# A scheduled two-layer hybrid block: triangular-solve inputs through DRAM, a fused key norm, and a last projection that closes row tile 0 first

## The chip, the cores and the metric

The kernel runs on one NeuronCore of one Trainium2 chip. The metric is device time in microseconds (us) of one execution, as the median of three runs. One further execution was profiled; every row below comes from that one.

## The reference, cut to what matters

Two layers work on 256 latent tokens (stream 1) and, in layer 0 only for the output, 256 context tokens (stream 0); the width is 2048 and everything is float32.

```python
h = rms_norm(x, pre_norm) * (1 + scale) + shift          # adaLN from c
p = split_columns(h @ w_in)                              # one input projection
att = gqa_block_attention(q, keys, vals) * silu(g)       # 8 heads, 8 rows of 128
S = S*w - (S@kk)(kk*a)^T + v k^T ; o = S@r               # RWKV-7 scan, both directions
kk = heads(k * k_k); kk = kk / max(|kk|, 1e-12)
y = concat([att, rwkv, pool]) @ w_out                    # one output projection
x = x + gate * rms_norm(y, post_norm)
```

The scan is computed in chunks of 64 tokens: within a chunk the recurrence becomes a triangular system whose 32x32 diagonal blocks are inverted by elimination.

## The kernel before, in words

The program is written by a scheduler in Python. About twenty workers (generators: `scan`, `front`, `back`, `elim`, `fin`, `att`, `mix`, `main`, `w_split`, `post`, loads ...) yield instructions. `Scheduler.run` keeps a planned clock for each engine, takes the instruction that can start first by that clock (with a priority by worker), and issues it. The order that comes out is fixed: on the chip each engine runs its own list in order and waits at semaphores. All DMAs are issued by SyncE (SP), so SP's list is one queue too.

What the planner believes of a DMA stands in `Engine.call` and `run`: its size is counted in bytes, it holds SP for 60 ns, moves 350 bytes per ns through one pipe, and lands 2900 ns after that (`DMA_LATENCY`); the next engine sees it 130 ns later.

```python
self.free_at["D"] = s + 60
st = max(self.dma_free, s + 60)
self.dma_free = st + op.dur / 350.0
end = self.dma_free + DMA_LATENCY
```

TensorE (PE) carries the projections. Every weight tile `wf` is split into a rounded high part by ScalarE (ACT) and a low part by VectorE (DVE), both in tiles of class `sp`, and each product is made of three matmuls into PSUM (`acc`). `main_in` and `main_out` make these; they have the lowest priority and fill what the other workers leave of PE. Buffers are slots of pools; `CLASSES` gives the most tiles of a class and `PHASES` how many are kept for it at each stage of the run.

Around that runs the RWKV work in 16 units (2 layers x 4 channel groups x 2 streams). `front` makes decays and keys, `back` makes the chunk matrices on PE (`pr<-rf`), masks them on DVE into `UB` (`rb<-pr,c`) and `W`, and copies the diagonal 32x32 blocks with ACT into `N0` (8 copies, `tp<-rb`). `elim` turns `N0` into the layout of the elimination with two DVE transposes into the one tile `DT` (`dt<-tp`), runs 31 steps of a product and an addition (`tp<-dt,tp` and `tp<-tp`), and transposes the result into `T1` and `T2`. `fin` copies those back (`rb<-tp` on ACT) and multiplies them (`pr<-tp,rb` and `pr<-tp` on PE), and `scan` runs the chunks.

The last output projection is `main_out(1, 1, 0)` and `main_out(1, 1, 1)`: 16 k-tiles for columns 0 to 1023 and both row tiles of 128 tokens, then the same for columns 1024 to 2047. `post_work(1, 1)` takes each finished PSUM tile (times the gate on DVE, squares on ACT), and after all eight of them sums the squares, makes the inverse root for both row tiles (12 small DVE steps), then does eight `SCALAR_TENSOR_TENSOR` with the residual and eight stores.

Of the kernel before, what the change touches and what calls it, by code (L numbers as in the profile page):

```python
# [15 lines left out]
ALU = mybir.AluOpType  # L16
# [85 lines left out]
def layout(a):  # L102
# [22 lines left out]
CLASSES = {  # L125
# [15 lines left out]
}  # L141
# [29 lines left out]
def STEPS():  # L171
    into = [[("in", l, g) for g in range(len(GROUPS(l)))] for l in range(DEPTH)]
    out = [("out", 0, 0, 0), ("out", 0, 0, 1), ("out", 0, 1, 0)]
    return into[0] + out + into[1][:EARLY] + [("out", 0, 1, 1)] + into[1][EARLY:] + [("out", 1, 1, 0), ("out", 1, 1, 1)]

# [31 lines left out]
BACK = 60.0  # L207
HELD = 121.75
HOLD = {None: 1000.0, "ada": 3000.0}
# [418 lines left out]
class Hybrid:  # L628
    def __init__(self, ctx, tc, a, log=None):
        self.ctx, self.tc, self.nc, self.a = ctx, tc, tc.nc, a  # L630
        nc = self.nc
        self.V, self.S, self.G = Engine("V", nc.vector), Engine("S", nc.scalar), Engine("G", nc.gpsimd)
        self.T, self.D = Engine("T", nc.tensor), Engine("D", nc.sync)
        pool = lambda n, **kw: ctx.enter_context(tc.tile_pool(name=n, bufs=1, **kw))
        sb, ps = pool("sb"), pool("ps", space=PSUM)
        fixed = sum(n * TILES[t] for t, n in COUNT.items() if t != "p")
        slots = (SB_BYTES - CONST_BYTES - fixed) // TILES["b"]
        tiles = {t: (ps if t == "p" else sb, COUNT.get(t, slots), size) for t, size in TILES.items()}
        self.cp = pool("const")
# [8 lines left out]
        self.ygd = [dram("ygd%d" % l, [4, 128, 512]) for l in range(DEPTH)]  # L648
        self.sch = Scheduler(tiles, CLASSES, log)
        self.sch.set_phase(PHASES["start"])  # L650
        self.flags = set()
        self.now = "start"
        self.count = {}
# [6 lines left out]
    def phase(self, name, after=None):  # L660
        def go():
            if after in (None, self.now):
                self.now = name
                self.sch.set_phase(PHASES[name])
        self.sch.defer(go)

# [167 lines left out]
    def w_loads(self):  # L834
        yield self.until("loaded")
        for kind, l, *at in STEPS()[1:]:
            if kind == "in":
                for q in range(4):
                    for _, _, cb, _, bs in GROUPS(l)[at[0]]:
                        yield from self.w_tile(l, cb, bs, q)  # L840
            else:
                for k in KMIX:
# [275 lines left out]
    def main_work(self):  # L1118
        left = {s: sum(s in STREAMS[m] for g in GROUPS(1) for *_, m, _ in g) for s in range(2)}
        for kind, l, *at in STEPS():  # L1120
            if kind == "in":
                yield from self.main_in(l, at[0], left)
            else:
                yield from self.main_out(l, *at)
# [59 lines left out]
    def main_out(self, l, s, nh):  # L1184
# [19 lines left out]
        if nh == 1:  # L1204
            self.free(*self.mx[l, s][0].values(), *self.mx[l, s][1].values())

    def emit(self, l, kind, i, ps, mode):
# [83 lines left out]
    def fin_work(self):  # L1291
        yield self.until("consts")
        for _ in range(DEPTH * 8):
            yield Until(lambda: len(self.zq) > 0)
            yield from self.fin(*self.zq.pop(0))

    def front(self, l, g, s, up):
# [14 lines left out]

        kr = yield Alloc("tp", (128, 256))
        yield V.tensor_scalar(out=kr, in0=k, scalar1=self.vec(l, "rw_k_k", g), scalar2=None, op0=ALU.mult)
        sq = yield Alloc("tp", (128, 256))
        yield S.activation(out=sq, in_=kr, func=AF.Square)
# [3 lines left out]
        yield V.tensor_tensor(out=kk, in0=kr, in1=psb[:, 0:256], op=ALU.mult)  # L1320
        self.free(kr, psb)

# [90 lines left out]
    def back(self, l, g, s, need, RS, W, BK, PC, bv):  # L1413
# [13 lines left out]
        for d in range(2):  # L1427
# [9 lines left out]
            for p in range(2):  # L1437
# [5 lines left out]
                self.free(psA[p])  # L1443
        N0 = yield Alloc("tp", (128, 2, 4, 32))
        for q in range(4):
            b = q % 2
            for d in range(2):
                yield S.copy(out=N0[Q[q], d], in_=UB[d][Q[q], :, 0, 32 * b:32 * b + 32])
        for d in range(2):
# [4 lines left out]
            self.free(psW)  # L1454
        self.push(self.bq, (N0, (l, g, s, need, RS, W, UB, BK, PC, bv)))

    def elim(self, N0, unit):
        V = self.V
        DT = yield Alloc("dt", (128, 2, 32, 32))
        for d in range(2):  # L1460
            src = N0[:, d].rearrange("p c t -> p t c").unsqueeze(2).to_broadcast([128, 32, 8, 4])
            dst = DT[:, 0].rearrange("p a b -> p b a") if d == 0 else DT[:, 1]
            yield V.transpose(out=dst, in_=src)
        self.free(N0)
# [3 lines left out]
        yield V.tensor_copy(out=ZZ, in_=z0)  # L1468
        for t in range(31, 0, -1):
            m0 = t // 8  # L1470
            M = 4 - m0
            tm = TM[:, 0:2 * t * M].rearrange("p (d a m) -> p d a m", d=2, a=t)
            yield V.tensor_tensor(out=tm, in0=DT[:, :, 0:t, t:t + 1].to_broadcast([128, 2, t, M]),
                                  in1=ZZ[:, :, t:t + 1, m0:4].to_broadcast([128, 2, t, M]), op=ALU.mult)
            yield V.tensor_tensor(out=ZZ[:, :, 0:t, m0:4], in0=ZZ[:, :, 0:t, m0:4], in1=tm, op=ALU.add)
        self.free(DT, TM)
# [9 lines left out]
    def fin(self, T1, T2, l, g, s, need, RS, W, UB, W2, PC, bv):  # L1486
        V, S, G, T = self.V, self.S, self.G, self.T
        for q in range(4):
            b = q % 2
            yield S.copy(out=UB[0][Q[q], :, 0, 32 * b:32 * b + 32], in_=T1[Q[q], 0].rearrange("p c u -> p u c"))  # L1490
            yield S.copy(out=UB[1][Q[q], :, 0, 32 * b:32 * b + 32], in_=T2[Q[q], 1])
        psY = yield Alloc("pr", (128, 512))
        for u in range(4):
            for p in range(2):
                q0, q1 = Q[2 * p], Q[2 * p + 1]
                o = slice(32 * u, 32 * u + 32)
                yield T.matmul(out=psY[q1, o], lhsT=UB[0][q0, u, 0, 32:64], rhs=T2[q0, 0, u, :], start=True, stop=True)
                yield T.matmul(out=psY[q0, o], lhsT=UB[1][q1, u, 0, 0:32], rhs=T1[q1, 1, :, u], start=True, stop=True)
        YS = yield Alloc("tp", (128, 4, 32))
# [3 lines left out]
        for u in range(4):  # L1503
            for p in range(2):
                q0, q1 = Q[2 * p], Q[2 * p + 1]
                o = slice(32 * u, 32 * u + 32)
                yield T.matmul(out=psZ[q0, o], lhsT=YS[q1, u, :], rhs=T1[q1, 0, :, u], start=True, stop=True)
                yield T.matmul(out=psZ[q1, o], lhsT=YS[q0, u, :], rhs=T2[q0, 1, u, :], start=True, stop=True)
        psz3 = psZ[:, 0:128].rearrange("p (u t) -> p u t", u=4)
# [3 lines left out]
        self.free(psZ, YS, T1, T2)  # L1513
        self.push(self.pq, (l, g, s, need, RS, W, UB, W2, PC, bv))

    def scan_work(self):
        yield self.until("consts")
        state = {}
        for _ in range(DEPTH * 8):
# [3 lines left out]
            if u[0:3] == (0, 3, 1):  # L1523
                self.phase("rested", "first")

    def scan(self, Sc, l, g, s, need, RS, W, UB, W2, PC, bv):
# [150 lines left out]
    def att_work(self, first):  # L1677
        yield self.until("consts")
        for l in range(first, DEPTH):
            while self.count.get(("att", l), 0) < 8:  # L1680
# [10 lines left out]
                if self.count["qdone", l, i // 4] == 4:  # L1691
                    self.free(*self.kf[l, i // 4], *self.vf[l, i // 4])

    def gate_work(self):
# [193 lines left out]
    def run(self):  # L1888
# [24 lines left out]
        sch.add("mix", PRIO["mix"], self.mix_work())  # L1913
        for l in range(DEPTH):
            for s in PASSES(l):
                sch.add("post%d%d" % (l, s), PRIO["post"], self.post_work(l, s), 16)
        sch.add("load", PRIO["load"], self.loads())
# [25 lines left out]
```

## Time and profile before

| what | value |
|---|---|
| median of 3 runs | 1725.89 us (1724.2 to 1728.25) |
| the profiled execution | 1729.24 us, of which the span from the first to the last instruction is 1727.4 us |
| PE, DVE, ACT busy | 1657.9, 1348.7, 929.0 us |
| granted TensorE clock | 0.987 of full speed |
| DMA | 349.77 MB, 61.4% of 16 engines' span on SP's queue |

PE is busy in 96% of the span. Of the rest, 18.5 us lie at the start, before the first weights land, and some 13 us at the end, after the last matmul.

### The profile page before, as it was taken

Reading aid. Unit: us, or ns where it says so; the run is one execution under the profiler, and the core shown is the slowest. Engines: PE = TensorE matmul, PEld = TensorE weight load, DVE = VectorE, ACT = ScalarE, POOL = GpSimd, SP = SyncE. Lnnn points to the kernel's source line nnn. Section 1 sums busy time; section 2 is a strip of 40 time slices with the busy share of each in tenths; the row PEclk is TensorE's granted clock in tenths of the full one; section 3 lists DMA queues with packets and bytes.
Section 4 is the critical chain, followed back from the end, with each engine's and each line's share of the span. In section 5 each row is a group of like instructions: output and inputs, shape, how many; then the busy total and the mean of one; then the engine's idle time right before and its main releaser. Section 6 shows DMA issues by size and latency. Waiting matters only on the chain.

```text
span 1727.4 us, 38237 instructions
## 1 busy us (share of the span) xinstructions
PE 1657.9 (96%) x13658; PEld 1336.4 (77%) x13658; DVE 1348.7 (78%) x4250; ACT 929.0 (54%) x2279; POOL 9.3 (1%) x77
## 2 busy tenths in 40 slices
PE   4899999999999999999999999989999999999997
PEld 3677676776777777777777889789999988998885
DVE  4335889898898898854557685899999999999663
ACT  5333454544555555534346574666546757766461
POOL 0000000000000000000000000000000000000000
PEclk9999999999999999999999999999999999999998
DMA  9993763567566655568579964574523554564762
GB/s 330 374 364 104 248 198 102 178 205 230 162 190 184 218 186 182 178 205 297 193 238 361 331 214 156 160 259 142 160 87 125 167 152 150 178 186 151 259 199 98
DMA packets 217822, 349.77 MB, mean 202 GB/s; under 512 B 22880, under 2 KB 61856, under 8 KB 217632
## 3 DMA queue, kind: packets, MB, share of 16 engines
q1 hardware_dynamic: 217632, 347.34, 61.4%
q8 instruction: 107, 1.75, 0.4%
q14 instruction: 83, 0.68, 0.1%
HBM read 316.41 MB, written 30.83 MB: 201 GB/s over the span
## 4 chain that ended last, share of the span: by engine, by line
PE 76%; DVE 10%; DMA 9%; ACT 2%; issue 2%; SPq 1%; DVEq 0%; ACTq 0%
PE acc L588 54%; PE pr L588 6%; PE att L588 6%; PE scan L588 5%; PE ada L588 4%; DVE tp L588 3%; DMA wa<-in_ada_w_dram 2%; DVE sp L588 2%; DMA w<-in_ada_w_dram 2%; DMA wf<-in_w_in_dram 2%; DVE rf L588 1%; DMA pw<-in_w_in_dram 1%; DVE dt L588 1%; PE st L588 1%; SPq L588 1%
## 5 line engine op out<-in xcount | busy, mean ns | idle before, releaser
L588 PE MATMUL acc<-h,sp 128*128 128x256 f32 (+1 forms) x5088 | 971.2, 339 | 11.4 <-DVE h L588 4.3
L588 PEld LDWEIGHTS acc<-h,sp 128*128 128x128 f32 x5088 | 759.1, 189 | 124.9 <-issue 11.6
L588 DVE TENSOR_TENSOR sp<-wf,sp 128x512 fp32r<-128x512 f32 (+1 forms) x568 | 359.4, 661 | 38.0 <-ACT sp L588 31.9
L588 ACT CAST sp<-wf 128x512 fp32r<-128x512 f32 (+1 forms) x624 | 351.3, 604 | 21.5 <-PE acc L588 5.7
L588 PE MATMUL acc<-sp,h 128*128 128x512 f32 x1152 | 278.4, 398 | 0.1
L588 PEld LDWEIGHTS acc<-sp,h 128*128 128x128 f32 x1152 | 215.0, 189 | 50.1 <-DVE sp L588 1.0
L588 DVE TENSOR_TENSOR tp<-tp 128x60 f32<-128x60 f32 (+21 forms) x552 | 134.4, 246 | 7.1 <-ACT tp L588 0.3
L588 DVE TENSOR_TENSOR tp<-dt,tp 128x48 f32<-128x48 f32 (+23 forms) x496 | 111.0, 224 | 6.3
L588 PEld LDWEIGHTS scan<-rf 128*64 128x64 f32 x1344 | 57.2, 138 | 34.6 <-issue 9.5
L588 PE MATMUL scan<-rf 128*64 128x64 f32 x1344 | 78.0, 233 | 1.7 <-DVE rf L588 1.0
L588 PE MATMUL ada<-wa,cs 128*2 128x256 f32 x1024 | 71.9, 378 | 2.5 <-DMA wa<-in_ada_w_dram 2.2
L588 ACT CAST pw<-pw 128x512 fp32r<-128x512 f32 x56 | 34.8, 622 | 65.4 <-DMA pw<-in_w_in_dram 59.8
L588 DVE TENSOR_TENSOR rf<-tp 64x256 f32<-64x256 f32 x176 | 69.2, 419 | 0.2
L588 DVE STREAM_TRANSPOSE dt<-tp 128x1024 f32<-128x1024 f32 x32 | 65.8, 2075 | 0.1
L588 DVE TENSOR_TENSOR pw<-pw 128x512 f32<-128x512 f32 x56 | 38.4, 686 | 34.5 <-ACT pw L588 34.2
L588 ACT ACTIVATE aq<-att,q 128x512 f32<-128x512 f32 (+1 forms) x48 | 34.0, 708 | 57.0 <-DVE q L588 40.7
L588 DVE COPY adasb<-ada 2x128 f32<-2x128 f32 (+1 forms) x32 | 11.4, 357 | 66.0 <-ACT adasb L588 63.9
L588 DVE SCALAR_TENSOR_TENSOR q<-q 128x4 f32<-128x4 f32 (+3 forms) x378 | 56.9, 155 | 3.7
L588 PE MATMUL ada<-w,cs 128*2 128x128 f32 x1024 | 37.5, 295 | 21.2 <-DMA w<-in_ada_w_dram 20.2
L588 ACT COPY rf<-scan 64x128 f32<-64x128 f32 x128 | 33.3, 260 | 44.1 <-PE scan L588 40.6
L588 ACT COPY adasb<-ada 2x128 f32<-2x128 f32 (+1 forms) x32 | 9.9, 309 | 87.2 <-PE ada L588 83.7
L588 ACT COPY sm<-scan 128x128 f32<-128x128 f32 x64 | 17.1, 267 | 69.6 <-PE scan L588 69.1
(153 smaller groups left out, 1936.6 us busy)
## 6 DMA issues: line engine op xcount, KB each, us to landing
wf<-in_w_in_dram SPq DMA_DIRECT2D x384, 256.0 KB, 3.6
wa<-in_ada_w_dram SPq DMA_DIRECT2D x256, 256.0 KB, 4.6
wf<-in_w_out_dram SPq DMA_DIRECT2D x192, 256.0 KB, 4.7
w<-in_ada_w_dram SPq DMA_DIRECT2D x128, 256.0 KB, 5.4
pw<-in_w_in_dram SPq DMA_DIRECT2D x56, 256.0 KB, 4.5
w<-pw SPq DMA_DIRECT2D x56, 256.0 KB, 2.5
sp<-w SPq DMA_DIRECT2D x56, 256.0 KB, 3.5
wf<-in_w_in_dram SPq DMA_DIRECT2D x48, 128.0 KB, 4.6
```

The lines of the kernel that those rows point to most:

```text
L588: op.call(**op.args)
```

## The change

1. `back` no longer copies the diagonal blocks with ACT: SP stores them to one of four DRAM tiles `nd` (8 DMAs a unit). `elim` no longer transposes on DVE: SP loads `DT` from `nd`, replicated over the partitions (16 DMAs a unit). The second direction's elimination now runs in mirrored index order, so that its access patterns change and `T1` and `T2` change places for it.
2. `front` folds the key scale into the squaring on ACT and into the product with the norm on DVE; one DVE instruction a unit goes.
3. The last output projection becomes `main_end`: fourteen k-tiles for columns 0 to 1023, the same fourteen for columns 1024 to 2047, both row tiles, then the last two k-tiles for all columns of row tile 0, then those of row tile 1, from eight weight tiles that are held. `post_last` prefetches the residual and normalises each row tile by itself.
4. When a worker's last unit is done, what the phases keep for its classes is set to zero (`done`); classes `y` and `sp` may grow to 24 and 30 tiles; the planner's cost `HELD` is 120 instead of 121.75.

```diff
+ENDING = [[(k, n) for k in KMIX[:14] for n in (0, 1)] + [(k, n) for n in (2, 3) for k in KMIX[:14]], [(k, n) for n in range(4) for k in KMIX[14:]]]
-HELD = 121.75
+HELD = 120
...
+        for late in range(2):
+            for k, n in ENDING[late]:
...
+                for t in range(2 - late):
+                    yield from product(k, n, t, h, w)
...
+        for k, n, h, w in held:
+            yield from product(k, n, 1, h, w)
...
+            for n in range(4):
+                yield V.scalar_tensor_tensor(out=y[n], in0=y[n], scalar=rs, in1=xr[n], op0=ALU.mult, op1=ALU.add)
...
-                yield S.copy(out=N0[Q[q], d], in_=UB[d][Q[q], :, 0, 32 * b:32 * b + 32])
+                yield D_.dma_start(out=nd[q, d].rearrange("c s t -> s c t"), in_=UB[d][Q[q], :, 0, 32 * b:32 * b + 32])
...
-            yield V.transpose(out=dst, in_=src)
+        for q in range(4):
+            for c in range(4):
+                src = nd[q, :, c].rearrange("d s t -> d (s t)").unsqueeze(0).to_broadcast([8, 2, 1024])
+                yield self.D.dma_start(out=DT[32 * q + c:32 * q + 32:4].rearrange("p d s t -> p d (s t)"), in_=src)
```

The order on DVE at the twelfth unit (layer 1, the first unit of stream 1), from the last mask (`rb<-pr,c`) to the first that reads or writes `dt`; first before:

```order
L588 TENSOR_TENSOR rf<-pr,c 64x4x2x64
L588 TENSOR_TENSOR rb<-pr,c 64x512
L588 TENSOR_SCALAR q<-q 128x8
L588 TENSOR_TENSOR at<-at 128x512
L588 TENSOR_TENSOR sp<-wf,sp 128x512
L588 SCALAR_TENSOR_TENSOR q<-q 128x8
L588 STREAM_TRANSPOSE dt<-tp 128x32x32
L588 TENSOR_TENSOR sp<-wf,sp 128x512
L588 STREAM_TRANSPOSE dt<-tp 128x1024
```

and the same place in the changed kernel:

```order
L589 TENSOR_TENSOR rf<-pr,c 64x4x2x64 x2
L589 TENSOR_TENSOR rb<-pr,c 64x512
L589 COPY tp<-c 128x256
L589 TENSOR_TENSOR sm<-sm,scan 128x128
L589 TENSOR_TENSOR rf<-sm,q 64x2x64
L589 TENSOR_TENSOR sp<-wf,sp 128x512
L589 TENSOR_TENSOR sm<-sm,q 128x128
L589 TENSOR_TENSOR rf<-sm,q 64x2x64
L589 TENSOR_TENSOR sp<-wf,sp 128x512
L589 TENSOR_TENSOR tp<-dt,tp 128x62
```

The transposes are gone, and seven instructions stand between the last mask and the first step that needs `DT`.

SP's list for that unit in the changed kernel (`nd` is the DRAM tile, `wf` a weight tile); before, SP had nothing to do with a unit's elimination:

```order
L589 DMA wf<-in_w_in_dram 128x512 x5
L589 DMA rkvd_72<-ev 128x256
L589 DMA nd_133<-rb 32x4x32 x8
L589 DMA wf<-in_w_in_dram 128x512
L589 DMA dt<-nd_133 8x2x1024 x8
L589 DMA wf<-in_w_in_dram 128x512
L589 DMA dt<-nd_133 8x2x1024 x8
L589 DMA wf<-in_w_in_dram 128x512
```

Twenty-four DMAs have come in among the weights' loads.

The end of DVE's list, from the last evacuations of PSUM (`y<-acc,y`) on; before:

```order
L588 TENSOR_TENSOR y<-acc,y 128x512 x4
L588 TENSOR_REDUCE q<-q 128x2
L588 TENSOR_SCALAR q<-q 128x2 x3
L588 SCALAR_TENSOR_TENSOR q<-q 128x2
L588 TENSOR_TENSOR q<-q 128x2
L588 SCALAR_TENSOR_TENSOR q<-q 128x2 x2
L588 TENSOR_TENSOR q<-q 128x2
L588 SCALAR_TENSOR_TENSOR q<-q 128x2 x2
L588 TENSOR_TENSOR q<-q 128x2
L588 SCALAR_TENSOR_TENSOR q<-q 128x2
L588 SCALAR_TENSOR_TENSOR y<-y,q 128x512 x8
```

and in the changed kernel, from the evacuation of row tile 1's last columns on:

```order
L589 TENSOR_TENSOR y<-acc,y 128x512
L589 SCALAR_TENSOR_TENSOR q<-q 128x1 x2
L589 TENSOR_TENSOR q<-q 128x1
L589 SCALAR_TENSOR_TENSOR q<-q 128x1
L589 SCALAR_TENSOR_TENSOR y<-y,q 128x512
L589 TENSOR_REDUCE q<-q 128x1
L589 SCALAR_TENSOR_TENSOR y<-y,q 128x512 x3
L589 TENSOR_SCALAR q<-q 128x1 x3
L589 SCALAR_TENSOR_TENSOR q<-q 128x1
L589 TENSOR_TENSOR q<-q 128x1
L589 SCALAR_TENSOR_TENSOR q<-q 128x1 x2
```

All four evacuations of row tile 1 stand ahead of row tile 0's four `y<-y,q`; the 12 small steps of row tile 1 follow behind these (the last five are not shown), and its four `y<-y,q` end the list.

## Rows read from the trace of the kernel before

**Rows 1.** The page: busy us, share of the span and instructions of each engine
```profile
PE 1657.9 (96%) x13658; PEld 1336.4 (77%) x13658; DVE 1348.7 (78%) x4250; ACT 929.0 (54%) x2279; POOL 9.3 (1%) x77
```

**Rows 2.** Waits of PE: us in total, times, longest us
```profile
PE pr L588 <- ACT tp L588: 4.2, 5, 2.4
PE acc L588 <- DVE sp L588: 2.8, 5, 1.1
...
PE pr L588 <- DVE tp L588: 0.4, 1, 0.4
```

**Rows 3.** Windows over the eliminations of layer 0 and layer 1, engines' busy us
```profile
225.00:725.00 500.00, 491.89 (x4296) 359.93 (x4295) 451.00 (x1561) 261.87 (x684) 3.81 (x34) 1.00 0.58 184
1125.00:1575.00 450.00, 440.89 (x4308) 407.13 (x4307) 427.90 (x1493) 295.25 (x760) 2.90 (x24) 0.99 0.50 160
```

**Rows 4.** The end of the chain of waits: start us, us, what
```profile
1641.45 72.37 PE acc L588 x311
...
1715.73 0.69 DVE y L588
...
1716.52 0.18 DVE q L588
...
1718.89 0.75 DVE y L588
```

**Rows 5.** The page: the transposes into DT, busy, mean ns, idle before
```profile
L588 DVE STREAM_TRANSPOSE dt<-tp 128x1024 f32<-128x1024 f32 x32 | 65.8, 2075 | 0.1
```

**Rows 6.** ACT's groups by form: the copies into N0
```profile
L588 ACT COPY tp<-rb 32x128 f32<-32x128 f32 x128 | 37.6, 295 | 20.0 <-DVE rb L588 18.2
```

**Rows 7.** Timeline of ACT, second unit: the copies that fin's matmuls read
```profile
300.77 1.25 ACT L588 COPY rb<-tp 32x128 f32<-32x128 f32 x4
302.67 1.24 ACT L588 COPY rb<-tp 32x128 f32<-32x128 f32 x4
```

**Rows 8.** Timeline of PE, second unit: fin's first matmuls
```profile
302.03 0.29 PE L588 MATMUL pr<-tp,rb 32*32 32x32 f32 x4
304.80 0.64 PE L588 MATMUL pr<-tp,rb 32*32 32x32 f32 x28
```

**Rows 9.** Loads of 64 KB, tile tu: ns of an issue min/median/max; landing
```profile
L588 SPq DMA_DIRECT2D tu<-in_rw_w_up_dram x16: 371/424/1631, 144.7 to 1459.8; - x16
...
DMA to landing us min/median/max: 2.0/3.0/5.0
```

**Rows 10.** Timeline of SP: the first loads, one behind the other
```profile
2.11 3.75 SPq L588 DMA_DIRECT2D y<-in_ctx_dram  x8
```

**Rows 11.** DMA issues of the first 3 us: KB each, us to landing
```profile
c<-in_consts_dram SPq DMA_DIRECT2D x1, 64.0 KB, 2.4
tl<-in_cond_dram SPq DMA_DIRECT2D x1, 16.0 KB, 1.6
```

**Rows 12.** Waits of SP's queue: us in total, times, longest us
```profile
SPq L588 <- PE acc L588: 275.7, 216, 6.1
```

**Rows 13.** DVE's groups by form: what stands between mask and elimination
```profile
L588 DVE TENSOR_TENSOR sp<-wf,sp 128x512 fp32r<-128x512 f32 x520 | 340.3, 684 | 34.7 <-ACT sp L588 29.0 <-DMA w<-in_ada_w_dram 3.6
...
L588 DVE TENSOR_TENSOR rf<-sm,q 64x128 f32<-64x128 f32 x96 | 27.2, 283 | 1.4
L588 DVE TENSOR_TENSOR sm<-sm,q 128x128 f32<-128x128 f32 x56 | 15.6, 279 | 0.2
L588 DVE COPY tp<-c 128x256 f32<-128x256 f32 x16 | 4.6, 285 | 0.0
```

**Rows 14.** PE's groups by form: the input projections of layers 0 and 1
```profile
L588 PE MATMUL acc<-h,sp 128*128 128x512 f32 x2208 | 577.8, 405 | 8.1 <-DVE h L588 4.3 <-DVE sp L588 1.8 <-ACT sp L588 1.5
L588 PE MATMUL acc<-h,sp 128*128 128x256 f32 x2880 | 393.4, 288 | 3.3 <-DMA sp<-w 2.3 <-DVE sp L588 1.0
```

**Rows 15.** Timeline: the last unbroken stretch of PE, the last steps of DVE
```profile
1689.75 24.99 PE L588 MATMUL acc<-sp,h 128*128 128x512 f32 x107
1718.89 5.39 DVE L588 SCALAR_TENSOR_TENSOR y<-y,q 128x512 f32<-128x512 f32 x8
```

More of the change, by code (lines that the diff above doesn't have):

```diff
@@ L173, in STEPS @@
     out = [("out", 0, 0, 0), ("out", 0, 0, 1), ("out", 0, 1, 0)]
-    return into[0] + out + into[1][:EARLY] + [("out", 0, 1, 1)] + into[1][EARLY:] + [("out", 1, 1, 0), ("out", 1, 1, 1)]
+    return into[0] + out + into[1][:EARLY] + [("out", 0, 1, 1)] + into[1][EARLY:] + [("end", 1, 1)]
 def TILES_IN(l, gi):
@@ L648, in __init__ @@
         self.ygd = [dram("ygd%d" % l, [4, 128, 512]) for l in range(DEPTH)]
+        self.nd = [dram("nd%d" % i, [4, 2, 4, 32, 32]) for i in range(4)]
         self.sch = Scheduler(tiles, CLASSES, log)
@@ L652, in __init__ @@
         self.now = "start"
+        self.over = {}
         self.count = {}
@@ L664, in go @@
                 self.sch.set_phase(PHASES[name])
+                self.sch.set_phase(self.over)
         self.sch.defer(go)
@@ L840, in w_loads @@
                         yield from self.w_tile(l, cb, bs, q)
+            elif kind == "end":
+                for k, n in ENDING[0] + ENDING[1]:
+                    w = yield Alloc("wf", (128, 1, 512))
+                    yield self.D.dma_start(out=w[:, 0], in_=self.a["w_out"][l, 128 * k:128 * k + 128, 512 * n:512 * n + 512])
+                    self.push(self.wq, (w, None, 0))
             else:
@@ L1122, in main_work @@
                 yield from self.main_in(l, at[0], left)
+            elif kind == "end":
+                yield from self.main_end(l, *at)
             else:
@@ L1205, in main_out, with main_end, product @@
             self.free(*self.mx[l, s][0].values(), *self.mx[l, s][1].values())
+    def main_end(self, l, s):
+        T = self.T
+        self.nmain += 64
+        self.flag("end")
+        ps, held = {}, []
+        def product(k, n, t, h, w):
+            mh, ml = (self.mx[l, s][j][k // 2][:, k % 2, 128 * t:128 * t + 128] for j in range(2))
+            if (n, t) not in ps:
+                ps[n, t] = yield Alloc("acc", (128, 512))
+            yield T.matmul(out=ps[n, t], lhsT=mh, rhs=h[:, 0], start=(k == KMIX[0]), stop=False)
+            yield T.matmul(out=ps[n, t], lhsT=mh, rhs=w[:, 0], start=False, stop=False)
+            yield T.matmul(out=ps[n, t], lhsT=ml, rhs=h[:, 0], start=False, stop=(k == KMIX[-1]))
+        for late in range(2):
+            for k, n in ENDING[late]:
+                yield Until(lambda: len(self.sq) > 0)
+                h, w = self.sq.pop(0)
+                yield self.until("m", l, s, k // 2)
+                for t in range(2 - late):
+                    yield from product(k, n, t, h, w)
+                    if late and k == KMIX[-1]:
+                        self.sch.defer(lambda key=(l, s, n, t), p=ps[n, t]: self.yq.__setitem__(key, p))
+                if late:
+                    held.append((k, n, h, w))
+                else:
+                    self.free(h, w)
+        for k, n, h, w in held:
+            yield from product(k, n, 1, h, w)
+            self.free(h, w)
+            if k == KMIX[-1]:
+                self.sch.defer(lambda key=(l, s, n, 1), p=ps[n, 1]: self.yq.__setitem__(key, p))
+        self.free(*self.mx[l, s][0].values(), *self.mx[l, s][1].values())
@@ new lines, in post_last @@
+    def post_last(self):
+        V, S, G, T, D_ = self.V, self.S, self.G, self.T, self.D
+        l, s = DEPTH - 1, 1
+        yield self.until("end")
+        yield self.until("gp", l)
+        gp = []
+        for n in range(4):
+            g = yield Alloc("y", (128, 512))
+            src = self.gpd[l].rearrange("(k s) p -> s k p", s=2)[s, 4 * n:4 * n + 4, :]
+            yield D_.dma_start(out=g.rearrange("p (k c) -> p k c", k=4), in_=src.unsqueeze(0).to_broadcast([128, 4, 128]))
+            gp.append(g)
+        acc = yield Alloc("q", (128, 2, 4))
+        for t in range(2):
+            xr, y = [], []
+            rows = slice(128 * t, 128 * t + 128)
+            for n in range(4):
+                z = yield Alloc("y", (128, 512))
+                yield D_.dma_start(out=z, in_=self.x1d[rows, 512 * n:512 * n + 512])
+                xr.append(z)
+            for n in range(4):
+                yield Until(lambda: (l, s, n, t) in self.yq)
+                ps = self.yq.pop((l, s, n, t))
+                z = yield Alloc("y", (128, 512))
+                yield V.tensor_tensor(out=z, in0=ps, in1=gp[n], op=ALU.mult)
+                junk = yield Alloc("y", (128, 512))
+                yield S.activation(out=junk, in_=ps, func=AF.Square, accum_out=acc[:, t, n:n + 1])
+                self.free(junk, ps)
+                y.append(z)
+            ss = yield Alloc("q", (128, 1))
+            yield V.tensor_reduce(out=ss, in_=acc[:, t], axis=AX.X, op=ALU.add)
+            yield V.tensor_scalar(out=ss, in0=ss, scalar1=1.0 / D, scalar2=EPS, op0=ALU.mult, op1=ALU.add)
+            rs = yield from self.rsqrt(ss, 1)
+            for n in range(4):
+                yield V.scalar_tensor_tensor(out=y[n], in0=y[n], scalar=rs, in1=xr[n], op0=ALU.mult, op1=ALU.add)
+                self.free(xr[n])
+                yield D_.dma_start(out=self.a["out"][0, rows, 512 * n:512 * n + 512], in_=y[n])
+                self.free(y[n])
+            self.free(ss, rs)
+        self.free(acc, *gp)
@@ L1514, in fin, with done, go @@
         self.push(self.pq, (l, g, s, need, RS, W, UB, W2, PC, bv))
+    def done(self, **least):
+        def go():
+            self.over.update(least)
+            self.sch.set_phase(least)
+        self.sch.defer(go)
     def scan_work(self):
```

51 lines of the change are left out of this document (26 added, 25 removed), and 4 rows, old and new, of tables (CLASSES, PHASES).

## The prediction, written before the changed kernel ran

> **What bounds the kernel now.** I read the shares of the engines first: PE is busy 1657.9 of 1727.4 us, DVE 78%, ACT 54% [rows 1]. So time can only come from PE's gaps or from its own pace. The waits of PE came next: outside the start and the end they are small, 2.8 us for DVE's split weights, 4.2 and 0.4 us in the units' front part [rows 2]. Then the windows over the two stretches in which the eliminations run: PE 492 of 500 and 441 of 450 us, DVE 451 of 500 (90%) and 428 of 450 (95%) [rows 3]. DVE is nearly as full as PE there, but it seldom holds PE up. The chain of waits at the end is the third view: from 1641.45 on PE works without a break on the last projection for 72.4 us, and then DVE alone sets the end [rows 4]. No wait for a late k-tile is seen there, so closing columns or row tiles in another order fills no gap of PE; it can only change what follows the last matmul.
>
> **The change part by part.**
>
> *What goes from DVE and ACT.* The 32 transposes into `DT` are 65.8 us of DVE, 4.1 us in each of 16 units [rows 5], and the 128 copies into `N0` are 37.6 us of ACT [rows 6]; the key scale is one DVE step of 128x256 a unit, under 0.5 us. Both engines lie beside PE, so this is worth only what PE waits for them: 7.4 us in all [rows 2]. I take -2 us (bounds -7 and 0), because at the same places DVE gets a new wait.
>
> *What comes in its place.* A unit now has 24 DMAs on SP. SP needs 3.75 us for eight loads in a row, 0.47 us each [rows 10]; the load of a 64 KB tile holds it 0.42 us (at least 0.37) and lands after 3.0 us (2.0 to 5.0) [rows 9]. The planner that made the order counts 60 ns for an issue. By its own numbers the stretch from the last mask to `DT` is: two stores 0.12, 16 KB 0.05, landing 2.9, sixteen loads of 64 KB at 0.19 are 3.0, landing 2.9, and three steps from engine to engine of 0.13: 9.3 us. By the rows it is two stores and a weight load between 3 x 0.47 = 1.4, sixteen loads 16 x 0.47 = 7.5 and the last landing 3.0: 11.9 us. The stores' own landing, 1.6 us for 16 KB in 128 pieces of 128 bytes [rows 11], is hidden behind the first eight loads, which need earlier stores. From below: 0.74 for two stores, 16 x 0.371 = 5.9 and 2.0 are 8.7 us, which is inside the plan. From above: all eight stores late 3.8, 1.6, 7.5 and 5.0 are 17.9 us. So `DT` is late against the plan by 2.6 us by the median rows, by 0 at the low end, by 8.6 at the high end.
>
> What hides it on DVE is little: at the unit shown, seven steps stand between mask and elimination, 2 x 0.684 + 2 x 0.283 + 2 x 0.279 + 0.285 = 2.8 us [rows 13], so DVE, which takes its list in order, sits idle for some 9 us. Behind it wait the splits of weight tiles, and all of the elimination. Some 4 us of it is the time of the transposes that are gone; the rest is why I don't count on the relief above.
>
> Who feels it is PE, at `fin`'s first matmuls, since its list is fixed too. In the unit shown PE reaches them 0.01 us after the first four copies have ended (300.77 + 1.25 against 302.03), and the second set 0.9 us after (302.67 + 1.24 against 304.80) [rows 7, 8]. In 13 of the 16 units this margin is under 1 us, in the other three 1.5, 3.9 and 8.6. So the planner places PE's instructions about when their data come, and a delay that it does not know of arrives at PE less about 0.5 us. By the median rows that is 2.1 us a unit; between that and the low end, zero, I take the middle, 1.05 us, in 13 units: +14 us (bounds 0 and 16 x 8.6 = 138, the latter only if every unit meets the worst row).
>
> The Trainium skill ("DMA: Bandwidth & Descriptors", section "Anatomy of one DMA — SWDGE (gpsimd) path") puts the sequencer's dispatch of a DMA at about 50 ns, close to the planner's 60. By it the sixteen loads would take 0.8 us to issue and this term would be 0; the rows here show 0.42 to 0.47 us on SP's queue, and I go by them. The same page ("Specifications") says that transfers under 512 bytes are slow because they read, modify and write; the new stores have pieces of 128 bytes. The one load of that kind in this trace landed in 1.6 us, sooner than one of 64 KB in larger pieces (2.4) [rows 11], so I put no price on it.
>
> *PE's own list.* It holds 10,494 matmuls before and after, in 1430 rows of equal instructions before and 1452 now. What a break costs is bounded by layer 0's projection: 577.8 / 2208 = 0.262 us a matmul against 24.99 / 107 = 0.234 in an unbroken stretch [rows 14, 15], so 62 us over its 258 rows, 0.24 us each. 22 rows are 5 us at most; most new ones are attention's short products with the same array shape, so I take +2 (bounds 0 and 5).
>
> *The end.* The last evacuation on DVE starts at 1715.73 and the last `y<-y,q` ends at 1718.89 + 5.39 = 1724.28: 8.55 us [rows 4, 15]. Of these the 12 small steps take 1718.89 - 1716.52 = 2.37, 0.20 each, and the eight wide ones 0.67 each. In the changed list the last evacuation (0.69) is followed by four small steps left of row tile 0 (0.79), its four wide steps with a sum among them (2.7 + 0.2), twelve small ones (2.37) and four wide ones (2.7): 9.4 us. Closing row tile 0 first should save four wide steps behind the last matmul, -2.7 us; in the list that was made its small steps stand behind evacuations that wait for PE, so I take +0.8 us (bounds -2.7 and +1).
>
> *The sum.* -2 + 14 + 2 + 0.8 = +14.8 us. The profiled execution took 1729.24 us, 1.84 more than its span; that gives 1744.0. The median of the runs is 3.35 us lower, so the median should become 1741 us.
>
> **The rivals.**
>
> *A: the loads are hidden and the relief reaches PE.* If SP gets the loads off in 0.371 us and they land in 2 us, `DT` is there inside the plan (8.7 against 9.3 us), and DVE, at 90 to 95% before, has 4 us a unit left over. Then PE's 7.4 us of waits go and the end costs at most 0.8 us: some 1720 us, down to 1716 with the end as intended. For it: DVE really is the second engine, and SP mostly waits for others, 275.7 us for PE alone [rows 12], so its issue time may be free. Against it: the margin on PE is under 1 us in most units, and both rows that it needs are minima.
>
> *B: hidden, and nothing won.* PE's work is the same, 96% of the span, and the relief is on engines that wait for PE; the end's +0.8 and +2 for the breaks stand against -2: 1727 us. It needs the same low end as A, without the gain.
>
> *C: SP's list itself is too full.* 24 DMAs are 11.3 us of SP in a unit, in which the weights' loads stand in between. In layer 1 the low parts in `sp` are held to 11 tiles, 5 pairs, and a pair feeds twelve matmuls of 393.4 / 2880 = 0.137 us [rows 14]: 8.2 us in hand. If a unit's DMAs came in one block, PE would run dry for 3.1 us in each of 16 units, 50 us: 1776 us. It decides where the block is longer than the tiles in hand. Against it: the order puts weight loads between the two halves of most blocks, and in layer 0 a pair lasts twice as long.
>
> **How the numbers follow.** The forecast, slower by the chain through DRAM, gets 0.52, A 0.24, B 0.15, C 0.09. Its own range is 1730 to 1764: the low end a term of 4 us, the high end 2.1 us in all 16 units and the upper bounds of the other terms. For 8 times in 10 I reach to 1718 below, which holds B and the larger part of A, and stay at 1764 above, which leaves C out. What a measurement of this kernel can tell from no change is about 0.2%, 3.5 us: faster 0.24 (A), within 0.2 (B) 0.15, slower 0.61 (the forecast and C).
>
> **What would show it.** Right: idle time of DVE of 3 to 9 us before the first `tp<-dt,tp` of most units, put down to the load of `dt`; the sixteen loads about 0.4 us apart on SP; PE waiting 1 to 3 us a unit for ACT or DVE before `pr<-tp,rb`, far above the 4.2 and 0.4 us in total of [rows 2]; an end of about 9.4 us between the last evacuation and the last wide step. Wrong: no idle time before `tp<-dt,tp`, or idle time there with PE as unbroken as before; then DVE had nothing else to do and the wait is free (B), or PE's waits for DVE are gone (A). If PE instead waits before `acc<-h,sp` for weights, it is C. The prediction fails altogether if PE's mean time for a matmul changes, since I hold its work fixed.

## The result and the profile after

The changed kernel takes 1860.33 us (median of 4 runs, 1857.07 to 1861.74) against 1725.05 us (4 runs, 1723.57 to 1728.25) for the kernel before on the same chip: 1.0779 times as long, 95% interval 1.0757 to 1.0801. The direction of the forecast was right, its size was not: +135 us came instead of +15.

The page of the changed kernel gives the engines' busy time, and the chain that ended last by engine; [rows 1] is its counterpart.

```profile
PE 1686.1 (91%) x13658; PEld 1358.5 (73%) x13658; DVE 1300.1 (70%) x4216; ACT 904.4 (49%) x2152; POOL 9.0 (0%) x77
...
PE 65%; DMA 11%; DVE 10%; SPq 9%; ACT 3%; issue 2%; DVEq 0%; ACTq 0%
...
L589 DVE TENSOR_TENSOR tp<-dt,tp 128x48 f32<-128x48 f32 (+23 forms) x496 | 111.2, 224 | 112.8 <-DMA dt<-nd 67.3
```

DVE and ACT got relief, though less than was counted: they are busy 48.6 and 24.6 us less, where the transposes and copies that are gone had 65.8 and 37.6 [rows 5, 6]. PE pays. Its idle time, span less busy, was 69.5 us and is 171.5 (+102.0), and for the same 13,658 matmuls it is busy 28.2 us longer; that is the whole +130.2 us of the span (1857.6 against 1727.4). SP's queue, 1% of the chain before, is 9% of it, or 9% of 1857.6 = some 167 us. The last row names the place: 112.8 us in which DVE stood idle before the steps that read `DT`; before the change it was 6.3. Nearly all of it lies before the first of the 31 steps of a unit, the one of 62 columns, as DVE's group of that form shows, first before, then in the changed kernel (x16, then busy us, mean ns, idle us before):

```profile
L588 DVE TENSOR_TENSOR tp<-dt,tp 128x62 f32<-128x62 f32 x16 | 4.1, 253 | 0.0
```

```profile
L589 DVE TENSOR_TENSOR tp<-dt,tp 128x62 f32<-128x62 f32 x16 | 4.1, 258 | 105.8 <-DMA dt<-nd 67.3 <-DMA nd<-rb 22.4 <-DMA wf<-in_w_in_dram 8.5
```

That is 6.6 us a unit. The profile puts 11 of the 16 waits down to the loads of `dt` and five to other DMAs on SP's list; but in all 16 the step begins 1.7 to 2.9 us after the sixteenth load of `dt` was issued.

How long SP takes for the sixteen loads stands in the view of the tile `dt`: ns of one issue, least, median and most.

```profile
L589 SPq DMA_DIRECT2D dt<-nd x256: 643/656/1410, 229.8 to 1634.5; - x128
```

One issue is 0.656 us, where the 64 KB load of [rows 9] took 0.424. The timelines of SP, PE and DVE at the second unit show what follows from it (start us, us, what; in brackets the idle time before and what ended it).

```profile
267.31 11.20 SPq L589 DMA_DIRECT2D dt<-nd  x16
...
271.63 2.80 PE L589 MATMUL acc<-h,sp 128*128 128x512 f32 x11
281.88 0.47 PE L589 MATMUL att<-c,aq 128*128 128x128 f32 x1 [7.45 <-DVE aq L589]
...
274.38 0.16 DVE L589 TENSOR_SCALAR q<-q 128x4 f32<-128x4 f32 x1
280.75 0.26 DVE L589 TENSOR_TENSOR tp<-dt,tp 128x62 f32<-128x62 f32 x1 [6.20 <-DMA dt<-nd]
280.92 0.15 DVE L589 RECIPROCAL q<-q 128x1 f32<-128x1 f32 x1
280.99 0.41 DVE L589 TENSOR_TENSOR at<-at,ta 128x256 f32<-128x256 f32 x1
281.31 0.26 DVE L589 TENSOR_TENSOR tp<-tp 128x62 f32<-128x62 f32 x1
281.48 0.35 DVE L589 TENSOR_SCALAR aq<-aq,q 128x256 f32<-128x256 f32 x1
...
309.85 0.45 PE L589 MATMUL pr<-tp,rb 32*32 32x32 f32 x32
```

Read it in this order. SP is 11.20 us in sixteen issues, 0.70 us from one to the next; DVE finishes what it can at 274.54 and then stands 6.20 us at the first step of the elimination. Behind that step its list holds, among the steps of the elimination, the steps of attention's norm, the last of which makes `aq`. PE's next matmul reads `aq`, so PE stands 7.45 us. `fin`'s own matmuls, where the prediction looked for the wait, come 28 us later and start without a gap.

The waits of PE (us in total, times, longest us) say the same of all units; compare [rows 2].

```profile
PE acc L589 <- DVE sp L589: 20.9, 6, 7.2
...
PE pr L589 <- ACT tp L589: 17.6, 6, 7.5
PE att L589 <- DVE aq L589: 15.7, 5, 7.5
PE acc L589 <- DMA sp<-w: 14.8, 2, 8.5
PE ada L589 <- DMA wa<-in_ada_w_dram: 14.7, 8, 5.0
...
PE pr L589 <- DVE rf L589: 8.3, 2, 7.2
...
PE att L589 <- DVE q L589: 7.1, 1, 7.1
```

Seven kinds of consumer, stopped for up to 5.0 to 8.5 us at a time. No single operand is late: whatever stands behind the stalled step on DVE is, or behind the sixteen loads on SP, as the loads of `wa` and the two of `sp<-w`. In time the two stalls go together: in 15 of the 16 units a gap of PE of over 2.3 us begins while DVE stands, and these gaps are 93 us in sum.

The busy time grew because the clock fell. Windows of the changed kernel over its eliminations and around the gap above (us, then busy us of PE, PEld, DVE, ACT, POOL, then PE's granted clock, DMA share, GB/s); [rows 3] had 1.00 and 0.99:

```profile
225.00:725.00 500.00, 449.52 (x3813) 326.61 (x3805) 378.70 (x1351) 214.95 (x547) 3.58 (x33) 0.94 0.55 175
...
1150.00:1675.00 525.00, 467.12 (x4384) 422.78 (x4383) 430.55 (x1552) 292.54 (x725) 3.36 (x28) 0.94 0.50 157
...
270.00:274.00 4.00, 4.00 (x44) 3.07 (x43) 3.33 (x14) 3.89 (x10) 0.11 (x1) 1.00 0.39 111
274.00:282.00 8.00, 0.55 (x3) 0.12 (x2) 1.79 (x9) 0.51 (x3) 0.00 (x0) 0.68 0.50 154
282.00:286.00 4.00, 4.00 (x44) 3.21 (x45) 3.54 (x11) 2.44 (x7) 0.00 (x0) 0.50 0.25 93
286.00:290.00 4.00, 4.00 (x30) 2.75 (x29) 2.70 (x15) 0.82 (x3) 0.00 (x0) 0.85 0.39 137
290.00:294.00 4.00, 4.00 (x51) 2.66 (x50) 3.70 (x16) 1.51 (x4) 0.00 (x0) 1.00 0.40 125
```

PE had worked without a break at 1.00, which is 2.4 GHz; during its gap the grant fell, the next 4 us ran at 0.50, which is 1.2 GHz, and by 290 it was back. Here a gap cost its own length and a stretch of half speed behind it. The eleven longest gaps between PE's first and last matmul, 5.03 to 8.46 us, all have such a stretch; by the trace's records of the granted clock PE was busy for 97.9 us at 0.50, and for 28.4 us before the change.

The end came as counted. The last evacuation starts at 1843.62 and the last wide step ends at 1850.02 + 2.74 = 1852.76: 9.14 us, against 9.4 predicted and 8.55 before. The timeline of DVE there:

```profile
1843.62 0.69 DVE L589 TENSOR_TENSOR y<-acc,y 128x512 f32<-128x512 f32 x1
...
1845.73 2.07 DVE L589 SCALAR_TENSOR_TENSOR y<-y,q 128x512 f32<-128x512 f32 x3
...
1850.02 2.74 DVE L589 SCALAR_TENSOR_TENSOR y<-y,q 128x512 f32<-128x512 f32 x4
```

### The profile page after: what moved, and what is told of

Its sections match the earlier page's. It is cut to its first block, busy times and chain, and to the rows that moved or that the text cites. A ratio compares the mean times of both kernels' runs of the same rounds, so it can differ in the third digit from the quotient of the medians.

```text
span 1857.6 us, 38575 instructions
## 1 busy us (share of the span) xinstructions
PE 1686.1 (91%) x13658; PEld 1358.5 (73%) x13658; DVE 1300.1 (70%) x4216; ACT 904.4 (49%) x2152; POOL 9.0 (0%) x77
## 4 chain that ended last, share of the span: by engine, by line
PE 65%; DMA 11%; DVE 10%; SPq 9%; ACT 3%; issue 2%; DVEq 0%; ACTq 0%
PE acc L589 47%; SPq L589 9%; PE att L589 5%; PE scan L589 5%; PE pr L589 4%; PE ada L589 4%; DVE tp L589 3%; DMA wa<-in_ada_w_dram 3%; DMA w<-in_ada_w_dram 2%; DVE sp L589 2%; DMA pw<-in_w_in_dram 1%; DMA wf<-in_w_in_dram 1%; DVE rf L589 1%; DMA dt<-nd 1%; DVE q L589 1%
## 5 line engine op out<-in xcount | busy, mean ns | idle before, releaser
L589 PE MATMUL acc<-h,sp 128*128 128x256 f32 (+1 forms) x5088 | 987.0, 342 | 40.4 <-DMA sp<-w 14.8
L589 PEld LDWEIGHTS acc<-h,sp 128*128 128x128 f32 x5088 | 771.8, 192 | 154.6 <-DVE sp L589 16.7
L589 DVE TENSOR_TENSOR sp<-wf,sp 128x512 fp32r<-128x512 f32 (+1 forms) x568 | 363.2, 663 | 75.1 <-ACT sp L589 66.4
L589 ACT CAST sp<-wf 128x512 fp32r<-128x512 f32 (+1 forms) x624 | 355.1, 603 | 62.8 <-DMA wf<-in_w_out_dram 22.3
L589 DVE TENSOR_TENSOR tp<-dt,tp 128x48 f32<-128x48 f32 (+23 forms) x496 | 111.2, 224 | 112.8 <-DMA dt<-nd 67.3
L589 DVE TENSOR_TENSOR tp<-tp 128x72 f32<-128x72 f32 (+21 forms) x552 | 134.0, 246 | 7.7 <-ACT tp L589 0.6
L589 PE MATMUL ada<-wa,cs 128*2 128x256 f32 x1024 | 77.1, 393 | 15.2 <-DMA wa<-in_ada_w_dram 14.7
L589 ACT COPY rf<-pr 64x128 f32<-64x128 f32 (+1 forms) x96 | 34.8, 369 | 52.3 <-PE pr L589 49.1
L589 PEld LDWEIGHTS ada<-wa,cs 128*2 128x2 f32 x1024 | 21.8, 84 | 49.1 <-DMA wa<-in_ada_w_dram 22.0
L589 PE MATMUL ada<-w,cs 128*2 128x128 f32 x1024 | 36.8, 292 | 20.7 <-DMA w<-in_ada_w_dram 19.7
L589 ACT COPY rb<-tp 32x128 f32<-32x128 f32 x128 | 47.6, 417 | 12.7 <-DVE tp L589 11.9
```

Of the source, the lines that this page charges most:

```text
L589: op.call(**op.args)
```

## The experiments

Theory: DVE stands at the first reader of `DT` because SP needs 0.70 us for an issue that the planner counts at 0.06, and PE, whose list is as fixed, stands with it. Rivals: another part of the change does the harm (the planner's number `HELD`, ns that it adds before an instruction of DVE, ACT or POOL that starts in another group of 32 partitions than the one before it; the last projection; the fused norm), or the path through DRAM is slow whatever is planned. The runs stand beside each other in this table, worked out from the page of each profiled execution (us; idle of PE is the span less PE busy):

| run | span | PE busy | PE idle | DVE idle before `tp<-dt,tp` |
|---|---|---|---|---|
| before | 1727.4 | 1657.9 | 69.5 | 6.3 |
| after | 1857.6 | 1686.1 | 171.5 | 112.8 |
| e1_rest | 1781.6 | 1682.5 | 99.1 | 7.0 |
| e2_dram | 1876.8 | 1704.0 | 172.8 | 125.4 |
| e3_pool | 1834.6 | 1685.7 | 148.9 | 96.6 |
| e5_thirtytwo | 2040.9 | 1705.8 | 335.1 | 266.1 |
| e6_held | 1745.3 | 1665.5 | 79.8 | 6.7 |
| e7_rest_held | 1733.3 | 1659.4 | 73.9 | 6.5 |
| e9_end | 1726.4 | 1657.6 | 68.8 | 6.2 |
| e8_plan | 1771.1 | 1671.6 | 99.5 | 26.2 |
| f1_told_before | 1734.4 | 1664.5 | 69.9 | 7.3 |
| f2_told_dram | 1770.6 | 1674.6 | 96.0 | 26.7 |
| f5_told_pool | 1808.1 | 1685.6 | 122.5 | 51.4 |
| f4_three | 1729.3 | 1659.7 | 69.6 | 6.2 |

**e1_rest: all of the change but the path through DRAM.**

```diff
-    back, elim, fin of the changed kernel
+    back, elim, fin of the kernel before
```

> All of the change but its path through DRAM: the diagonal blocks go by ACT's copies and DVE's transposes again. Theory 1 (DVE stands at the first step that reads DT while SP issues sixteen loads one by one, and PE stands for what is queued behind on DVE): 1718 to 1732 us, PE idle near 70 us in all, clock near 0.987, no idle time of DVE above 1 us put down to DT. Rival 1 (a good part of the loss is the rest of the change: larger pools, released reserves, the new last projection, the reordering): above 1760 us. Rival 2 (the data's way, not their issue, is what takes long): as theory 1.

Measured: 1776.2 us (1773.27 to 1783.38), ratio 1.0281 (1.0253 to 1.0309). Adding the path to it brings 84 us, but the rest isn't free either: 50 us. That is in rival 1's range, not in theory 1's. This asked for e6, e7 and e9, which take the rest apart.

**e2_dram: the kernel before with the path through DRAM alone.**

```diff
+        self.nd = [dram("nd%d" % i, [4, 2, 4, 32, 32]) for i in range(4)]
-    back, elim, fin of the kernel before
+    back, elim, fin of the changed kernel
```

> The kernel before with the path through DRAM alone. Theory 1 and rival 2: 1830 to 1880 us, DVE idle about 90 to 120 us before steps that read DT, PE's clock lower in the stretches with eliminations. Rival 1: below 1800 us.

Measured: 1878.65 us in one run, 152 above the kernel before. The path by itself is enough for all of the harm, and for slightly more than the whole change brings. DVE's idle time grew by 119.1 us and PE's by 103.3.

**e3_pool: the changed kernel, `dt`'s loads issued by POOL.**

```diff
-                yield self.D.dma_start(out=DT[...
+                yield self.P.dma_start(out=DT[...     # P: nc.gpsimd, planned as SP is
```

> The changed kernel, but POOL issues the sixteen loads of DT; SP keeps the eight stores. Theory 1: DVE's idle time before DT follows the issue time x of a load on POOL, by 16 times (x - 0.70) us a unit, and the weights' loads on SP are no longer held; with x at 0.4 us some 1780 us, with x at 0.7 about 1845, with x at 1.0 about 1940. Rival 2: DVE's idle time stays at 6 to 8 us a unit whatever x is, and the time at 1850 to 1860.

Measured: 1836.7 us in one run, 24 less. The view of the tile `dt` shows POOL's issue:

```profile
L589 POOL DMA_DIRECT2D dt<-nd x256: 551/551/791, 225.7 to 1610.8; - x128
```

Sixteen at 0.551 are 8.8 us, still above the 3.0 that the plan gives these loads, and DVE still stands 96.6 us. By theory 1's own scale 0.551 would give some 1813 us and 2.4 us a unit less of DVE's idle time; 1.0 a unit went. The run lies between theory and rival and does not decide between them. Part of what POOL's shorter issue saves is lost again: POOL stood 14.7 us in 16 waits between these loads until earlier ones had landed, and a load landed 4.3 us after its issue (median), where the plan has 2.9.

**e5_thirtytwo: the changed kernel, twice as many loads of half the size.**

```diff
-                src = nd[q, :, c]... .to_broadcast([8, 2, 1024])
-                yield self.D.dma_start(out=DT[32 * q + c:32 * q + 32:4]...
+                for d in range(2):
+                    src = nd[q, d, c]... .to_broadcast([8, 1024])
+                    yield self.D.dma_start(out=DT[32 * q + c:32 * q + 32:4, d]...
```

> The changed kernel with 32 loads of 32 KB for DT in place of 16 of 64 KB: the same bytes, twice the issues. Theory 1: some 10 us more in each of 16 units, 2000 to 2050 us, and DVE idle 250 to 300 us before DT. Rival 2: within 15 us of the changed kernel, 1860 us.

Measured: 2042.66 us in one run, 182 more than the changed kernel. The tile's view and the page's chain:

```profile
L589 SPq DMA_DIRECT2D dt<-nd x512: 602/603/1437, 229.1 to 1786.0; - x171
```

```profile
PE 59%; SPq 17%; DVE 11%; DMA 7%; issue 3%; ACT 3%; DVEq 0%; ACTq 0%
```

The bytes are the same; the issues are twice as many at 0.603 us, which adds 32 x 0.603 - 16 x 0.656 = 8.8 us a unit, 141 us in 16 units. DVE's idle time grew by 153.3 us, PE's by 163.6, and PE's busy time by 19.7. Time and idle time are both in theory 1's range. So it is the number of issues on SP, and not what they move, that sets the stall.

**e6_held: the kernel before with one planner's number changed.**

```diff
-HELD = 121.75
+HELD = 120
```

> The kernel before with the planner's cost HELD at 120 in place of 121.75 and nothing else: the same instructions in another order. Theory 3 (the 50 us that the rest of the change costs by itself are the order that the planner happens to find; any small nudge can cost tens of us): 1735 to 1790 us. Rival 3 (they come from the parts of the rest: pools, released reserves, last projection): 1720 to 1732 us.

Measured: 1747.22 us (1745.58 to 1752.88), ratio 1.0132 (1.0087 to 1.0177). No instruction is added or taken away, and it costs 21 us: PE is idle 10.3 us more and busy 7.6 us more. The prediction had no term for this edit.

**e7_rest_held: e1 with `HELD` at 121.75.**

```diff
-HELD = 120
+HELD = 121.75
```

> The rest of the change without the path through DRAM, with HELD back at 121.75. Theory 3: a time that may lie anywhere from 1715 to 1790 us, over 10 us away from the 1776 us that it took at 120, without the stretch of low clock and little weight traffic near 1420 to 1500. Rival 3: within 8 us of 1776.

Measured: 1732.2 us (1724.3 to 1735.08, 10 runs), ratio 1.0027 (1.0008 to 1.0046). So 44 of the 50 us of e1 hung on this number, and the rest of the change is worth some +6 us. Where they lie is seen in a window late in layer 1, first of e1, then of e7:

```profile
1350.00:1575.00 225.00, 198.73 (x2009) 173.94 (x2008) 198.27 (x745) 132.45 (x363) 1.50 (x15) 0.86 0.38 120
```

```profile
1350.00:1575.00 225.00, 221.82 (x2249) 204.57 (x2249) 214.72 (x811) 161.00 (x427) 1.50 (x15) 1.00 0.52 166
```

In e1 PE does 240 matmuls fewer in this stretch, at a clock of 0.86. Which step of the planner leads there stays open.

**e9_end: the kernel before with the new last projection alone.**

```diff
-    ... + [("out", 1, 1, 0), ("out", 1, 1, 1)]
+    ... + [("end", 1, 1)]
+    main_end, post_last, done and their buffers
```

> The kernel before with the new last projection, its normalisation by row tiles and what these need (released reserves, larger pools), HELD at 121.75, the key norm and the eliminations as before. By the sum of the prediction its own cost is +0.8 us at the end; if the order up to the end stays as it is, 1724 to 1729 us. Theory 3: any nudge moves the order and the time with it. Rival 3: 1760 us or more.

Measured: 1728.36 us (1721.92 to 1732.08, 10 runs), ratio 1.0009 (0.9991 to 1.0028). The end is 1719.17 + 2.74 - 1712.77 = 9.14 us here too. The new projection moves the time by nothing that can be told.

**e8_plan: the changed kernel, and the planner told what an issue takes.**

```diff
-                self.free_at["D"] = s + 60
-                st = max(self.dma_free, s + 60)
+                self.free_at["D"] = s + (700 if <a load of dt> else 450)
+                st = max(self.dma_free, s + (700 if <a load of dt> else 450))
```

> The changed kernel with the planner told what SP takes: 450 ns an issue, 700 ns for a load of DT. If it is the planner's ignorance that hurts, DVE's idle time before DT falls to under 40 us in all and the time to 1770 to 1810 us; if it is the length of the loads itself, which nothing can fill since other work is not there, DVE idles as before, 100 us or more, and the time stays at 1840 to 1870.

Measured: 1773.13 us in one run, 87 less than the changed kernel. SP's issues are as long as they were (0.656 us) and no DMA is taken away; the planner now places other work of DVE in front, and DVE's idle time before `tp<-dt,tp` falls from 112.8 to 26.2 us.

**f1_told_before: the kernel before, the planner told 450 ns for each issue.**

```diff
-                self.free_at["D"] = s + 60
-                st = max(self.dma_free, s + 60)
+                self.free_at["D"] = s + 450
+                st = max(self.dma_free, s + 450)
```

> The kernel before, with one number of the planner changed: it counts 450 ns of SP for each DMA issue, where it counted 60. Theory (the planner's ignorance of issue time harms only where an engine waits for a chain of many issues, as for the sixteen loads of dt): before has no such chain, so 1720 to 1735 us. Rival (any new number sets off another order, and a new order costs 20 us and more, as the change of HELD alone did): 1740 to 1770 us. Third possibility: the true cost lets it place weight loads better, PE's 69.5 us of idle time shrink by 5 us or more, and it is under 1720.

Measured: 1737.49 us (1735.59 to 1741.35), ratio 1.007 (1.0044 to 1.0097). Between theory and rival: the truer number made the kernel before slower by 0.7%. PE's idle time is unchanged (69.9 us), its busy time 6.6 us longer at a granted clock of 0.983 instead of 0.987. Why the new order draws a lower clock stays open.

**f2_told_dram: the kernel before with the path through DRAM, and the planner told.**

```diff
-    back, elim, fin of the kernel before
+    back, elim, fin of the changed kernel
-                self.free_at["D"] = s + 60
-                st = max(self.dma_free, s + 60)
+                self.free_at["D"] = s + (700 if <a load of dt> else 450)
+                st = max(self.dma_free, s + (700 if <a load of dt> else 450))
```

> The kernel before with the path through DRAM alone, as in the run that took 1878.65 us, and the planner told that an issue takes 450 ns of SP and a load of dt 700 ns. Theory (the harm of the path is that the planner believes dt is there 8 us before it is): 1750 to 1800 us, with under 40 us of idle time of DVE before tp<-dt (125.4 without the telling). Rival (it is the path itself, its latency and SP's time, and not what the planner believes): over 1840 us, with over 100 us of that idle time.

Measured: 1772.37 us in one run, as the theory had it; 106 us of the path's 152 are gone by telling alone. Against f1, which has the same planner, the path costs 35 us. The chain of waits of f2 by engine:

```profile
PE 69%; DVE 13%; DMA 9%; SPq 4%; ACT 2%; issue 2%; DVEq 0%; ACTq 0%
```

SP's queue, 1% of the chain in the kernel before, is still 4% of it. The true cost of the issues doesn't vanish; it is only no longer paid in full.

**f5_told_pool: the changed kernel, POOL's loads and the planner told 450 ns.**

```diff
-                yield self.D.dma_start(out=DT[...
+                yield self.P.dma_start(out=DT[...     # P: nc.gpsimd
-                self.free_at["D"] = s + 60
-                st = max(self.dma_free, s + 60)
+                self.free_at["D"] = s + 450
+                st = max(self.dma_free, s + 450)
```

> The changed kernel with dt's loads issued by POOL (551 ns each, measured) and the planner told 450 ns for each issue. Theory (planner's belief and issue time add up, and POOL's list is empty where SP's is full): under the 1773.13 us of the run that told the planner and kept the loads on SP, 1745 to 1768 us. Rival (once the planner knows, DVE finds other work and the engine that issues is worth nothing): 1770 to 1780 us. Either way idle time of DVE before tp<-dt under 50 us.

Measured: 1809.9 us in one run; theory and rival both missed, and DVE's idle time is a little above 50 us. DVE stands 51.4 us, 43.1 of it for `dt` in 13 waits, 3.3 us each. The planner was told 0.450 where POOL takes 0.551: sixteen loads come 1.6 us later than planned, and in e8 it was told 0.700 where SP takes 0.70. That fits the theory's form, a stall by as much as the plan is short, but it explains half of it. For the rest the trace has two parts: POOL stood 13.8 us in 14 waits for earlier loads of `dt` to land, some 0.9 us a unit, and a load landed 3.5 us after its issue (median), 0.6 later than the plan has it.

**f4_three: the new last projection with three k-tiles left to the end.**

```diff
-ENDING = [[... KMIX[:14] ...], [(k, n) for n in range(4) for k in KMIX[14:]]]
+ENDING = [[... KMIX[:13] ...], [(k, n) for n in range(4) for k in KMIX[13:]]]
```

> The kernel before with the new last projection, but three k-tiles left to the end instead of two. In the order that results, row tile 0's twelve small steps and four wide ones stand ahead of row tile 1's last two evacuations. Theory (the end is DVE's list behind the last matmul and nothing else): from the start of the last evacuation to the end of the last wide step 0.69 + 0.2 + 2.4 + 2.7 = 6.0 us, against 9.1 with two k-tiles and 8.55 before; the time 1725 us where the run with two took 1728, ratio to before 0.998 to 1.000. Rival (row tile 1's first evacuations and the small steps between them hold the accumulators and the last evacuation comes as much later): the stretch is 6.0 but the time stays at 1727 to 1729 us.

Measured: 1726.16 us (1720.07 to 1731.03, 12 runs), ratio 0.9995 (0.9981 to 1.0008). The timeline of PE's last matmuls and DVE's last steps:

```profile
1699.75 18.21 PE L589 MATMUL acc<-sp,h 128*128 128x512 f32 x78
...
1718.36 1.28 DVE L589 TENSOR_TENSOR y<-acc,y 128x512 f32<-128x512 f32 x2
...
1722.05 2.74 DVE L589 SCALAR_TENSOR_TENSOR y<-y,q 128x512 f32<-128x512 f32 x4
```

From PE's last matmul to the end of the span it is 1729.3 - 1717.96 = 11.3 us, where before has 1727.4 - 1714.75 = 12.7 and e9 1726.4 - 1712.74 = 13.7. Row tile 0's small steps now lie under PE, and the stretch behind PE is 1.3 us shorter than before; that is 0.08%, and the runs can't tell it from nothing. The stretch from the last evacuation on is some 5.8 us, where theory and rival both had 6.0; between their times the runs can't decide. This version and e9 are the two that can't be told from the kernel before, and none is faster.

## Why the prediction was wrong

**The failed step: "Who feels it is PE, at `fin`'s first matmuls".** The prediction found the late `DT`, the idle DVE and the fixed lists, and then asked only who reads what the elimination makes. It wrote that the splits of weight tiles wait behind DVE's stalled step, and gave them no price. PE was charged 1.05 us a unit for 13 units, 14 us. In fact the 6.6 us a unit that DVE stood came through almost whole: in the changed kernel DVE's idle time before `tp<-dt,tp` grew by 106.5 us and PE's idle time by 102.0; in e2, which has the path alone, by 119.1 and 103.3, in e5 by 259.8 and 265.6, in e3 by 90.3 and 79.4. `fin`'s own matmuls, where 1 to 3 us a unit were expected, have no gap in any unit, as PE's group of that form in the changed kernel shows (busy us, mean ns, idle us before):

```profile
L589 PE MATMUL pr<-tp,rb 32*32 32x32 f32 x512 | 10.7, 197 | 0.0
```

[rows 3] pointed that way: with DVE at 90 to 95% little can be made up behind a stall. That this is the reason was not tested by itself; e8 and f2 show that the same work in another order avoids most of the stall.

**The issue's size.** The term "sixteen loads 16 x 0.47 = 7.5" went by a burst of other loads [rows 10]; a load of `dt` takes 0.70, so 11.2, and the sign "about 0.4 us apart" missed with it. Even the upper end of the bounds kept 0.47 and spent its margin on landing and stores. With 11.2 the prediction's own sum makes 1.4 + 11.2 + 3.0 = 15.6 us where the plan has 9.3: `DT` is 6.3 us late instead of 2.6, and DVE did stand 6.6. Less the prediction's 0.5 that would be 5.8 us in 16 units, 93 us. So most of the number was lost here, and by taking the middle between 2.1 us and zero. That 93 comes near the 102.0 of PE is luck in part, since nothing waited at the place that was priced. (The range's high end has a slip too: with the upper bound 0 of the relief it is 1766 and not 1764.)

**The clock.** "The prediction fails altogether if PE's mean time for a matmul changes": it changed. PE's busy time at 0.50 grew by 69.5 us (97.9 against 28.4), and the same matmuls took 28.2 us longer, 28.2 of the 130.2. In most of the experiments too a longer idle time of PE goes with a longer busy time: +7.6 us in e6, +24.6 in e1, +46.1 in e2, +47.9 in e5. It isn't in proportion, and in f1 the busy time grew by 6.6 us with no more idle time.

**An edit without a term.** `HELD` got no price at all, and e6 shows 21 us for it. The prices don't add up (the path alone +152, `HELD` alone +21, the rest +6, all together +135). Each version gets an order of its own, which is the likely reason. How much of the 135 belongs to `HELD` when the path is there was not tried.

**What held.** Slower, by the chain through DRAM; idle time of DVE before `tp<-dt,tp` of 3 to 9 us, put down to `dt` (2.05 to 8.73 in the 16 units, 11 of them put down to it by the profile); the last stretch of 9.4 us (9.14), and that closing row tile 0 first saves nothing as ordered. Rival A's relief did arrive at DVE and ACT, but no run shows PE gaining by it. Rival C's gap, PE waiting for weights before `acc<-h,sp`, is there twice, 14.8 us, both times with the load of `sp<-w` issued behind a block of sixteen loads of `dt`; it is one of seven forms of the same stall. The terms of -2 for the relief and +2 for the breaks in PE's list were too small to be seen by themselves in any run. That the planner's 60 ns is behind most of the loss is shown by e8 and f2, one run each: with the number mended, 87 and 106 us go, with every DMA still there, and DVE's idle time before `tp<-dt,tp` falls with them, to 26.2 and 26.7 us. What remains, 47 us in e8 and 46 in f2, is not taken apart further than by f1.

## What to carry to other kernels

Where every engine runs a fixed list, price a late operand at everything that stands behind the waiting instruction, not at the readers of that operand: here, with DVE 90 to 95% busy, PE's idle time grew by 0.87 to 1.02 us for each us that DVE stood. Count DMAs by the issue time of their own shape, many small ones before few large ones, and give that number to whatever plans the order. A planner's constant is an edit like any other: it needs a term, or a run of its own.

## What was not expected of the hardware

- An issue on SP's queue took 0.656 us for 8 partitions of two rows of 1024 values, replicated from DRAM, and 0.603 for half of that; 0.424 for the plain 64 KB load of [rows 9]. Among these three the time follows the form of the load, hardly its bytes. The same load on POOL took 0.551; neither is near the planner's 0.060. The Trainium skill ("DMA: Bandwidth & Descriptors", section "Issuing engine by pattern") calls the path of sync and scalar generally the faster one. For the issue of this load the runs show POOL's 0.105 us shorter, and the kernel 24 us faster with it in a single run; but from the last issue to the first reader it is 1.7 to 2.9 us with SP in the changed kernel and 1.9 to 6.2 with POOL in e3.
- After a gap of 7.45 us PE's next 4 us ran at a granted clock of 0.50 and the 4 after that at 0.85; behind a gap of 5.03 us that ends at 520.97 it was 0.50 and 0.86 in the same way.
- The 128 stores of 16 KB in pieces of 128 bytes landed in a median of 1.7 us in e3 and 2.2 in f5, sooner than the 3.0 of the 64 KB loads of [rows 9].
